# Rotary embedding on one core: tiles of 4 to 12 rows per partition in contiguous runs, with three tables made by TensorE

## The chip, the cores and the metric

One Trainium2 chip, one of its NeuronCores. The metric is the device time of one execution in microseconds (us). The kernel before takes 161.24 us (median of three runs, 161.16 to 161.56).

## What is computed

`x` is 16 batches of 512 positions of 1024 floats, that is 16 heads of 64. Each head is split into halves x1 and x2 of 32, and every position has its own 32 cosines and sines:

```python
x = x.reshape(batch, seq, num_heads, head_dim)
x1, x2 = (x[..., :half_dim].copy(), x[..., half_dim:].copy())
cos = cos[None, :, None, :].copy()
sin = sin[None, :, None, :].copy()
rotated = np.concatenate([x1 * cos - x2 * sin, x1 * sin + x2 * cos], axis=-1)
```

Input and output have 33.55 MB each. A position takes three passes over its 1024 floats: t1 = x times cos, t2 = the swapped halves times (-sin, sin), and the addition of the two.

## The kernel before, in words

**Rows and tiles.** The 8192 positions are laid out as 64 rows u of 128 positions, one position per partition, 4 KB each. A tile is some rows per partition that are loaded and stored together. Batches 0, 1, 14 and 15 are tiles of 4 rows (a partition's piece is 16 KB, contiguous in memory); the other twelve batches go in pairs, six tiles of 8 rows, where a partition's piece is 32 KB and neighbouring partitions alternate between the two batches of the pair (`x2`, `o2`, L110, L111). The result is written over x in the buffer `x_sb`, a ring of 40 rows (RING, L43). The first 40 rows are loaded up front; a later tile goes where stored tiles lay.

**Tables.** cos and sin come into `stage` in the layout of a tile of 4 rows. The layout of a pair needs each position's partner row, so TensorE makes it: `pick`, a 0/1 matrix that ACT spreads out of the identity (L178), is multiplied with `stage` into `pair_ps` (L209). ACT writes the signed sine tables `s1_sb` and `s2_sb` (L183 to L188). VectorE (DVE) copies two small tables for its own use (L280, L281).

**Who does what in a row.** The order on each engine is written out by hand, with waits on semaphores; an engine executes its own list in order.
- DVE multiplies t1 into one of three slots (NT1) of `t1_ps` in PSUM (L302), one row ahead (LEAD) of the additions. Row u takes the slot of row u-3 and waits until that row has been added.
- GpSimd (POOL) makes t2 (L263), one or two rows at a time, and waits for the tile's load. Row 3 of each 8-row tile is made by DVE itself (L295, flag V2).
- The addition is done by DVE (L313), or for the rows flagged PE2 (rows 1, 3 and 5 of 8) by TensorE: it adds t2 into PSUM by a matmul with the identity (L225), and the scalar engine (ACT) copies the slot back to `x_sb` (L192). That copy is called the evacuation below.
- SP waits until the last row of a tile is added and issues its store (L162). Stores run on the DMA queue q1.
- ACT issues all loads (L154), on the queue q10. The loads beyond the ring stand in ACT's own list between its evacuations: after a certain row, ACT waits until the stores of the rows to be overwritten have landed (L195) and then issues the load. LAG (L70) sets the row: the tile of batch 10 after row 17, that of batch 12 after row 25, batches 14 and 15 after row 33.

```python
later.setdefault((b * R1 - RING) // R2 * R2 + R2 - 1 + LAG, []).append(t)
...
for u in range(NU):
    if PE2[u]:
        ae.wait_ge(sem_e, n_pe[u])
        ae.activation(xs[:, u % RING, :], t1_ps[:, u % NT1, :], COPY).then_inc(sem_a, 1)
    for t in later.get(u, ()):
        k = (tiles[t][0] * R1 - RING) // R2
        ae.wait_ge(sem_out[k], 16 * stores_of(k))
        load(ae, t)
```

Of the kernel before, what the change touches and what calls it, by code (L numbers as in the profile page):

```python
# [6 lines left out]
def bass_split_heads_rope_kernel(  # L7
# [32 lines left out]
    singles = (0, 1, batch - 2, batch - 1)  # L40
    tiles = [(b, R1 if b in singles else R2) for b in range(batch) if b in singles or b % 2 == 0]
    NT = len(tiles)
    RING = 5 * R2  # L43
# [3 lines left out]
    EARLY = (NU - RING) // R2  # L47
# [3 lines left out]
    PE2 = [R1 <= u < NU - R1 and u % R2 in (1, 3, 5) for u in range(NU)]  # L51
    V2 = [tiles[t][1] == R2 and r == V_ROW for t, r in rows]
# [17 lines left out]
    LAG = 10  # L70

    with ExitStack() as stack:
# [3 lines left out]
        s1_sb = stack.enter_context(nc.sbuf_tensor([P, R1, 2, HALF], fp32))  # L76
        s2_sb = stack.enter_context(nc.sbuf_tensor([P, R2, 2, HALF], fp32))
        ident = stack.enter_context(nc.sbuf_tensor([P, P], fp32))
        pick = stack.enter_context(nc.sbuf_tensor([P, 2, P // 2, 2], fp32))
        zero = stack.enter_context(nc.sbuf_tensor([P, BANK], bf16))  # L80
        tab_ps = stack.enter_context(nc.psum_tensor([P, BANK], fp32))
        pair_ps = stack.enter_context(nc.psum_tensor([P, 2, 2, R1, HALF], fp32))
# [15 lines left out]
        sem_g = stack.enter_context(nc.semaphore("pick"))  # L98
# [3 lines left out]
        c1_ps = tab_ps[:, 0:R1 * HALF].rearrange("p (r d) -> p r d", d=HALF)  # L102
        v_ps = tab_ps[:, R1 * HALF:R1 * HALF + HD].rearrange("p (t d) -> p t d", d=HALF)

        def c_of(t, r):
            return c1_ps[:, r, :] if tiles[t][1] == R1 else pair_ps[:, r // R1, 0, r % R1, :]

        x1 = x.rearrange("b (s r) d -> b s (r d)", r=R1)
        o1 = out.rearrange("b (s r) h d -> b s (r h d)", r=R1)
        x2 = x.rearrange("b (s r) d -> s b (r d)", r=R2)  # L110
        o2 = out.rearrange("b (s r) h d -> s b (r h d)", r=R2)  # L111
        xs = x_sb[:].rearrange("p n h t d -> p n (h t d)")

        def in_dram(single, pairs, t):
            b, n = tiles[t]
            return single[b] if n == R1 else pairs[:, b:b + 2, :]

        def in_sbuf(t):
            b, n = tiles[t]
            k = b * R1 % RING  # L120
            return x_sb[:, k:k + n].rearrange("p n h t d -> p (n h t d)")
# [5 lines left out]
        def swapped(k):  # L127
            return x_sb[:, k, :, ::-1, :]

        def over_heads(table):  # L130
            return table[:, None, :, :].broadcast_to([P, H, 2, HALF])
# [17 lines left out]
        def stores_of(k):  # L149

            return sum(b * R1 // R2 == k for b, _ in tiles)

        def load(eng, t):
            eng.dma_start(in_sbuf(t), in_dram(x1, x2, t)).then_inc(sem_in[t], 16)  # L154

        def on_sync(sp):
            for u in range(NU):
                t, r, k = where(u)
                if r == tiles[t][1] - 1:
                    wait_added(sp, u)  # L160
                    k = u // R2
                    sp.dma_start(in_dram(o1, o2, t), in_sbuf(t)).then_inc(sem_out[k] if k < EARLY else sem_rest, 16)  # L162
            sp.wait_ge(sem_rest, 16 * sum(stores_of(k) for k in range(EARLY, NU // R2)))

        def on_scalar(ae):
            later = {}
            for t, (b, n) in enumerate(tiles):
                if b * R1 + n <= RING:
                    load(ae, t)
                else:  # L170

                    later.setdefault((b * R1 - RING) // R2 * R2 + R2 - 1 + LAG, []).append(t)
                if t == 0:
                    for i, (table, sem) in enumerate(((cos, sem_cos), (sin, sem_sin))):
                        ae.dma_start(stage[:, i, :], table.rearrange("(s r) d -> s (r d)", r=R1)).then_inc(sem, 16)  # L175

            ae.wait_ge(sem_i, 2)
            ae.activation(  # L178
                pick[:], ident[:].rearrange("q (s k) -> q k s", k=2)[:, :, :, None].broadcast_to([P, 2, P // 2, 2]), COPY
            ).then_inc(sem_g, 1)  # L180
            ae.wait_ge(sem_sin, 16)
            sv = stage[:, 1, :].rearrange("s (r d) -> s r d", d=HALF)
            ae.activation(s1_sb[:, :, 0, :], sv, COPY, scale=-1.0)  # L183
            ae.activation(s1_sb[:, :, 1, :], sv, COPY).then_inc(sem_s, 1)
            ae.wait_ge(sem_t, 2)
            s2 = s2_sb[:].rearrange("p (k r) t d -> p k r t d", r=R1)
            ae.activation(s2[:, :, :, 0, :], pair_ps[:, :, 1, :, :], COPY, scale=-1.0)  # L187
            ae.activation(s2[:, :, :, 1, :], pair_ps[:, :, 1, :, :], COPY).then_inc(sem_s, 1)  # L188
            for u in range(NU):
                if PE2[u]:  # L190
                    ae.wait_ge(sem_e, n_pe[u])
                    ae.activation(xs[:, u % RING, :], t1_ps[:, u % NT1, :], COPY).then_inc(sem_a, 1)  # L192
                for t in later.get(u, ()):
                    k = (tiles[t][0] * R1 - RING) // R2
                    ae.wait_ge(sem_out[k], 16 * stores_of(k))  # L195
                    load(ae, t)

        def on_tensor(pe):
            pe.wait_ge(sem_z, 1)
            for k in range(NT1):  # L200
                for b in range(EH):
                    pe.matmul(  # L202
                        t1_ps[:, k, b * BANK:(b + 1) * BANK], zero[:, 0:P], zero[:], start=True, stop=True
                    ).then_inc(sem_w, 1)
            pe.wait_ge(sem_g, 1)
            pe.wait_ge(sem_cos, 16)
            pe.wait_ge(sem_sin, 16)
            for k in range(2):
                pe.matmul(  # L209
                    pair_ps[:, k].rearrange("p c r d -> p (c r d)"),  # L210
                    pick[:, k].rearrange("q s b -> q (s b)"),
                    stage[:].rearrange("q c f -> q (c f)"),
                    start=True,
                    stop=True,
                ).then_inc(sem_t, 1)
            for u in range(NU):
                if not PE2[u]:
                    continue
                pe.wait_ge(sem_m, u + 1)

                if not V2[u]:
                    pe.wait_ge(sem_p, n_pool[u])
                t2 = t2_sb[:, u % NT2, :, :, :].rearrange("p h t d -> p (h t d)")
                for b in range(EH):
                    ins = pe.matmul(  # L225
                        t1_ps[:, u % NT1, b * BANK:(b + 1) * BANK],
                        ident[:],
                        t2[:, b * BANK:(b + 1) * BANK],
                        start=False,
                        stop=True,  # L230
                        skip_group_check=True,
                    )
                ins.then_inc(sem_e, 1)

        def on_gpsimd(pl):
# [3 lines left out]
                out=ident[:],  # L239
                in_=ident[:],  # L240
# [3 lines left out]
                pattern=[[-1, P]],  # L244
                channel_multiplier=1,
            ).then_inc(sem_i, 1)
            for u in range(NU):
# [4 lines left out]
                if (t, r) == (0, 0):  # L252
                    pl.wait_ge(sem_s, 1)
                if (t, r) == (2, 0):
                    pl.wait_ge(sem_s, 2)
# [6 lines left out]
                table = (s1_sb if tiles[t][1] == R1 else s2_sb)[:, r:r + n]  # L262
# [7 lines left out]
        def on_vector(ve):  # L270
            ve.memset(zero[:], 0.0).then_inc(sem_z, 1)  # L271
            ve.wait_ge(sem_cos, 16)
            ve.tensor_copy(c1_ps, stage[:, 0, :].rearrange("s (r d) -> s r d", d=HALF)).then_inc(sem_c, 1)  # L273
# [3 lines left out]
            def pair_tables():  # L277
                ve.wait_ge(sem_s, 2)
                row = pair_ps[:, V_ROW // R1, 1, V_ROW % R1, :]
                ve.tensor_scalar_mul(v_ps[:, 0, :], row, -1.0).then_inc(sem_c, 1)  # L280
                ve.tensor_copy(v_ps[:, 1, :], row).then_inc(sem_c, 1)  # L281

            first_v = V2.index(True)

            def mul(u):
# [3 lines left out]
                if (t, r) == (2, 0):  # L289
                    pair_tables()  # L290
                if u == first_v:
                    ve.wait_ge(sem_c, 3)
                if V2[u]:
                    wait_t2_free(ve, u)
                    ve.tensor_tensor(t2_sb[:, u % NT2, :, :, :], swapped(k), over_heads(v_ps), mult)  # L295
                if u >= NT1:
                    v = u - NT1
                    if PE2[v]:
                        ve.wait_ge(sem_a, n_pe[v])  # L299
                    else:  # L300
                        ve.wait_ge(sem_v, n_comb[v])
# [7 lines left out]
            def comb(u):  # L309
                t, r, k = where(u)  # L310
                ve.wait_ge(sem_m, u + 1)
                ve.wait_ge(sem_p, n_pool[u])  # L312
# [51 lines left out]
```

## Time and profile before

| | |
|---|---|
| median of three runs | 161.24 us |
| span of the profiled execution, first to last instruction | 159.6 us |
| DVE busy | 129.6 us (81%), 117 instructions |
| POOL busy | 131.7 us (82%), 41 instructions |
| PE busy | 64.4 us (40%), mean granted clock 0.764 |
| ACT busy | 24.3 us (15%) |
| DMA | 67.25 MB in 3169 packets, mean 421 GB/s |
| one multiplication or addition of a row on DVE | 1.22 us, the next one starts 1.13 us after it |
| t2 on POOL, two rows / one row | 4.53 / 2.36 us |
| last store, issue to landing | 7.7 us |

The span is what the profiler saw of one execution; the 1.6 us between it and the median lie outside its first and last instruction. In the profile's rows of 40 slices each digit is the busy share of 4 us in tenths. In the timeline a row is start, duration, engine, line and operation, and in brackets how long the engine was idle before it and what released it. "ACTq" and "SPq" are instructions that issue transfers or wait in the sequencer; "issue" as releaser means that the profile shows nothing the engine waited for.

### The profile page before, as it was taken

The numbers are of one execution on the slowest core, as the hardware profiler recorded it, in microseconds if no ns is written. First come the engines' busy times: TensorE is split into PE (matmuls) and PEld (weight loads), VectorE is DVE, ScalarE is ACT, GpSimd is POOL, SyncE is SP. The second block draws the span as 40 slices with busy tenths as digits, with TensorE's granted clock in tenths as the row PEclk, the third lists the DMA queues.
The fourth block names the chain that finished last, engine by engine and source line by source line (L and its number), as shares of the span: only waits on it lengthen the run. The fifth ranks groups of instructions, "written<-read, shape, count | busy, mean of one in ns | idle before, by whom it ended". The sixth has DMA issues, their size and how long they took to land.

```text
span 159.6 us, 499 instructions
## 1 busy us (share of the span) xinstructions
PE 64.4 (40%) x94; PEld 22.2 (14%) x94; DVE 129.6 (81%) x117; ACT 24.3 (15%) x27; POOL 131.7 (82%) x41
## 2 busy tenths in 40 slices
PE   6050017076408870789067400575058506900000
PEld 1020011021102220222021100211021102300000
DVE  0069947999999989998999629999999999556900
ACT  0420002004300250023102040023202310220000
POOL 1069999999999999999999798992999999089400
PEclk9999999759985589557759985589957995585555
DMA  5999999999999999999999999999999999999997
GB/s 144 396 466 472 394 411 431 448 476 402 394 448 406 495 419 402 476 435 402 443 435 435 394 476 435 402 460 394 427 456 448 443 394 423 472 419 435 386 456 300
DMA packets 3169, 67.25 MB, mean 421 GB/s; under 512 B 352, under 2 KB 608, under 8 KB 608
## 3 DMA queue, kind: packets, MB, share of 16 engines
q10 hardware_dynamic: 1728, 33.69, 49.8%
q1 hardware_dynamic: 1440, 33.56, 48.9%
q14 instruction: 1, 0.01, 0.0%
HBM read 33.69 MB, written 33.55 MB: 421 GB/s over the span
## 4 chain that ended last, share of the span: by engine, by line
DMA 61%; DVE 17%; POOL 5%; PE 5%; issue 4%; ACTq 1%; ACT 1%; DVEq 0%; POOLq 0%; SPq 0%
DMA x_sb<-in_x_dram 43%; DMA out_dram<-x_sb 18%; DVE t_ps L302 8%; DVE x_sb L313 7%; POOL t_sb L263 5%; PE t_ps L225 5%; DVE t_sb L295 2%; ACT x_sb L192 1%; ACTq L154 1%; ACTq L175 1%; DVE tab_ps L280 0%; DVEq L312 0%; DVE tab_ps L281 0%; DVEq L299 0%; POOLq L259 0%
## 5 line engine op out<-in xcount | busy, mean ns | idle before, releaser
L263 POOL TENSOR_TENSOR t_sb<-x_sb,s_sb 128x2048 f32<-128x2048 f32 (+1 forms) x35 | 131.0, 3784 | 17.1 <-DMA x_sb<-in_x_dram 8.3
L225 PE MATMUL t_ps<-t_sb,ident 128*128 128x512 f32 x84 | 59.6, 857 | 69.1 <-DVE t_ps L302 56.7
L302 DVE TENSOR_TENSOR t_ps<-x_sb,pair_ps 128x1024 f32<-128x1024 f32 x48 | 57.5, 1221 | 5.2 <-ACT x_sb L192 5.2
L313 DVE TENSOR_TENSOR x_sb<-t_ps,t_sb 128x1024 f32<-128x1024 f32 x43 | 52.2, 1216 | 5.9 <-POOL t_sb L263 5.9
L192 ACT ACTIVATE x_sb<-t_ps 128x1024 f32<-128x1024 f32 x21 | 21.4, 1024 | 107.6 <-PE t_ps L225 99.9
L225 PEld LDWEIGHTS t_ps<-t_sb,ident 128*128 128x128 f32 x84 | 20.3, 267 | 108.2 <-DVE t_ps L302 78.7
L302 DVE TENSOR_TENSOR t_ps<-x_sb,tab_ps 128x1024 f32<-128x1024 f32 x16 | 19.2, 1222 | 2.6 <-DMA x_sb<-in_x_dram 2.5
L295 DVE TENSOR_TENSOR t_sb<-x_sb,tab_ps 128x1024 f32<-128x1024 f32 x6 | 7.3, 1209 | 0.0
L273 DVE COPY tab_ps<-stage 128x128 f32<-128x128 f32 x1 | 0.3, 296 | 7.6 <-DMA stage<-in_cos_dram 7.6
L209 PE MATMUL pair_ps<-stage,pick 128*128 128x256 f32 x4 | 2.0, 667 | 5.1 <-DMA stage<-in_sin_dram 5.1
L202 PE MATMUL t_ps<-zero 128*128 128x512 bf16 x6 | 2.7, 629 | 1.3 <-DVE zero L271 1.3
L178 ACT ACT_TABLE_LOAD x1 | 1.3, 1283 | 5.5 <-issue 5.5
L209 PEld LDWEIGHTS pair_ps<-stage,pick 128*128 128x128 f32 x4 | 1.2, 324 | 6.1 <-issue 6.0
L202 PEld LDWEIGHTS t_ps<-zero 128*128 128x128 bf16 x6 | 0.7, 136 | 2.4 <-DVE zero L271 1.2
L271 DVE MEMSET zero<- 128x256 uint32 x1 | 0.3, 272 | 0.9 <-PEq L346 0.9
L187 ACT ACTIVATE s_sb<-pair_ps 128x256 f32<-128x256 f32 x1 | 0.4, 384 | 1.7 <-PE pair_ps L209 1.7
L183 ACT ACTIVATE s_sb<-stage 128x128 f32<-128x128 f32 x1 | 0.3, 310 | 1.8 <-DMA stage<-in_sin_dram 1.8
L236 POOL MEMSET ident<- 128x128 f32 x1 | 0.2, 205 | 0.3 <-POOLq L346 0.3
L178 ACT ACTIVATE pick<-ident 128x256 f32<-128x256 f32 x1 | 0.4, 416 | 0.0
L188 ACT ACTIVATE s_sb<-pair_ps 128x256 f32<-128x256 f32 x1 | 0.4, 377 | 0.0
L238 POOL TENSOR_SCALAR_AFFINE_SELECT ident<-ident 128x128 f32<-128x128 f32 x1 | 0.3, 295 | 0.1
L346 POOL MEMSET const-float32-0.0<- 128x1 f32 x1 | 0.1, 99 | 0.3 <-issue 0.3
(6 smaller groups left out, 1.0 us busy)
## 6 DMA issues: line engine op xcount, KB each, us to landing
x_sb<-in_x_dram ACTq DMA_DIRECT2D x6, 4096.0 KB, 38.7
out_dram<-x_sb SPq DMA_DIRECT2D x6, 4096.0 KB, 25.3
x_sb<-in_x_dram ACTq DMA_DIRECT2D x4, 2048.0 KB, 22.7
out_dram<-x_sb SPq DMA_DIRECT2D x4, 2048.0 KB, 16.1
stage<-in_cos_dram ACTq DMA_DIRECT2D x1, 64.0 KB, 7.5
stage<-in_sin_dram ACTq DMA_DIRECT2D x1, 64.0 KB, 7.2
```

The source lines that it names most:

```text
L154: eng.dma_start(in_sbuf(t), in_dram(x1, x2, t)).then_inc(sem_in[t], 16)
L175: ae.dma_start(stage[:, i, :], table.rearrange("(s r) d -> s (r d)", r=R1)).then_inc(sem, 16)
L178: ae.activation(pick[:], ident[:].rearrange("q (s k) -> q k s", k=2)[:, :, :, None].broadcast_to([P, 2, P // 2, 2]), COPY).then_inc(sem_g, 1)
L187: ae.activation(s2[:, :, :, 0, :], pair_ps[:, :, 1, :, :], COPY, scale=-1.0)
L192: ae.activation(xs[:, u % RING, :], t1_ps[:, u % NT1, :], COPY).then_inc(sem_a, 1)
L202: pe.matmul(t1_ps[:, k, b * BANK:(b + 1) * BANK], zero[:, 0:P], zero[:], start=True, stop=True).then_inc(sem_w, 1)
L209: pe.matmul(pair_ps[:, k].rearrange("p c r d -> p (c r d)"), pick[:, k].rearrange("q s b -> q (s b)"), stage[:].rearrange("q c f -> q (c f)"),
L225: ins = pe.matmul(t1_ps[:, u % NT1, b * BANK:(b + 1) * BANK], ident[:], t2[:, b * BANK:(b + 1) * BANK], start=False, stop=True, skip_group ...
L263: pl.tensor_tensor(t2_sb[:, u % NT2:u % NT2 + n], x_sb[:, k:k + n, :, ::-1, :], table[:, :, None, :, :].broadcast_to([P, n, H, 2, HALF]), ...
L295: ve.tensor_tensor(t2_sb[:, u % NT2, :, :, :], swapped(k), over_heads(v_ps), mult)
L302: ve.tensor_tensor(t1_ps[:, u % NT1, :].rearrange("p (h d) -> p h d", d=HALF), x_sb[:, k, :, :, :].rearrange("p h t d -> p (h t) d"), c_of ...
L313: ve.tensor_tensor(xs[:, k, :], t1_ps[:, u % NT1, :], t2_sb[:, u % NT2, :, :, :].rearrange("p h t d -> p (h t d)"), add,).then_inc(sem_v, 1)
```

## The change

The 64 rows become eight tiles of 4, 8, 8, 8, 12, 12, 8 and 4 rows, called tiles 0 to 7 in the following. Each tile is one contiguous run of positions across batch borders, and a partition's piece is 16, 32 or 48 KB, contiguous. The ring stays at 40 rows, so tiles 0 to 4 are loaded up front; tile 5 lies over tiles 0 and 1, tile 6 over tile 2, tile 7 over rows of tile 3. The late loads stand after rows 17, 25 and 33 (LATE), and each waits for the stores of the tiles under it. Loads 0 to 7 and stores 0 to 7 are those of the tiles.

In a tile of 8 rows a partition now holds 8 successive positions, in one of 12 rows 12, so with the tiles of 4 rows three table layouts are needed. The identity is laid out three times side by side, and TensorE multiplies its columns with a stride of 2 or 3 by `stage`. The tables of the 8-row tiles go through the third slot of `t1_ps`, those of the 12-row tiles through `tab_ps`. TensorE adds rows 1, 3 and 5 of an 8-row tile and rows 1, 3, 5 and 9 of a 12-row tile, 20 rows in all (21 before). On DVE the waits for its own earlier additions are dropped, and a multiplication waits for the multiplication before it.

The diff, cut to its core:

```diff
-    singles = (0, 1, batch - 2, batch - 1)
-    tiles = [(b, R1 if b in singles else R2) for b in range(batch) if b in singles or b % 2 == 0]
-    RING = 5 * R2
+    sizes = (R1, 2 * R1, 2 * R1, 2 * R1, 3 * R1, 3 * R1, 2 * R1, R1)
+    starts = [sum(sizes[:t]) for t in range(len(sizes))]
+    tiles = list(zip(starts, sizes))
+    RING = 10 * R1
...
-    EARLY = (NU - RING) // R2
+    over = [[j for j in range(t) if tiles[j][0] < u0 + n - RING and u0 - RING < tiles[j][0] + tiles[j][1]] for t, (u0, n) in enumerate(tiles)]
+    EARLY = 1 + max(max(o) for o in over if o)
...
-    PE2 = [R1 <= u < NU - R1 and u % R2 in (1, 3, 5) for u in range(NU)]
-    V2 = [tiles[t][1] == R2 and r == V_ROW for t, r in rows]
+    ON_PE = {R1: (1,), 2 * R1: (1, 3, 5), 3 * R1: (1, 3, 5, 9)}
+    PE2 = [0 < t < NT - 1 and r in ON_PE[tiles[t][1]] for t, r in rows]
+    V2 = [tiles[t][1] > R1 and r == V_ROW for t, r in rows]
...
-    LAG = 10
+    LATE = {5: 17, 6: 25, 7: 33}
...
+        def pieces(flat, t):
+            u0, n = tiles[t]
+            return flat[u0 * P:(u0 + n) * P, :].rearrange("(p r) d -> p (r d)", r=n)
...
         def load(eng, t):
-            eng.dma_start(in_sbuf(t), in_dram(x1, x2, t)).then_inc(sem_in[t], 16)
+            eng.dma_start(in_sbuf(t), pieces(xf, t)).then_inc(sem_in[t], 16)
...
-            ae.wait_ge(sem_i, 2)
-            ae.activation(
-                pick[:], ident[:].rearrange("q (s k) -> q k s", k=2)[:, :, :, None].broadcast_to([P, 2, P // 2, 2]), COPY
-            ).then_inc(sem_g, 1)
...
+            ae.wait_ge(sem_t, 1)
+            signed(2 * R1, spread_ps[:, :, 1])
+            ae.activation(two_ps.rearrange("p (j r) d -> p j r d", r=R1), spread_ps[:, :, 0], COPY).then_inc(sem_s, 1)
+            signed(3 * R1, group_ps[:, 2:3, 1], 2).then_inc(sem_s, 1)
             ae.wait_ge(sem_t, 2)
+            signed(3 * R1, group_ps[:, 0:2, 1]).then_inc(sem_s, 1)
...
-                for t in later.get(u, ()):
-                    k = (tiles[t][0] * R1 - RING) // R2
-                    ae.wait_ge(sem_out[k], 16 * stores_of(k))
-                    load(ae, t)
+                for t in range(NT):
+                    if LATE.get(t) == u:
+                        for j in over[t]:
+                            ae.wait_ge(sem_out[j], 16)
+                        load(ae, t)
...
+            for j in range(2):
+                spread(2 * R1, j, spread_ps[:, j])
+            spread(3 * R1, 2, group_ps[:, 2]).then_inc(sem_t, 1)
+            pe.wait_ge(sem_m, R1)
+            for j in range(2):
+                ins = spread(3 * R1, j, group_ps[:, j])
+            ins.then_inc(sem_t, 1)
...
-                if u >= NT1:
-                    v = u - NT1
-                    if PE2[v]:
-                        ve.wait_ge(sem_a, n_pe[v])
-                    else:
-                        ve.wait_ge(sem_v, n_comb[v])
+                if u >= NT1 and PE2[u - NT1]:
+                    ve.wait_ge(sem_a, n_pe[u - NT1])
+                if u >= 1 and not (u >= NT1 and PE2[u - NT1] and PE2[u - 1]):
+                    ve.wait_ge(sem_m, u)
```

## The prediction

> **What bounds the kernel now.** I read the page's engine and DMA rows first, then the DMA view by windows, then the timeline of DVE and ACT around the later loads, then the chain. On the page, the 40 slices and the queue rows:
>
> ```profile
> DVE  0069947999999989998999629999999999556900
> POOL 1069999999999999999999798992999999089400
> DMA  5999999999999999999999999999999999999997
> q10 hardware_dynamic: 1728, 33.69, 49.8%
> q1 hardware_dynamic: 1440, 33.56, 48.9%
> ```
>
> The DMA engines are full from the second slice to the last but one: loads (q10, issued by ACT) and stores (q1, by SP) take 49.8 + 48.9 = 98.7% of 16 engines. DVE and POOL have holes, and these cost nothing while a store waits in its queue. So this kernel is bound by bytes, and anything that leaves both queues empty adds to the time one for one.
>
> The DMA view of 26 to 37 us, when stores in 16 KB pieces run beside loads in 32 KB pieces:
>
> ```profile
> q10 hardware_dynamic: 96, 3.15, 66.6%
> q1 hardware_dynamic: 100, 1.64, 34.7%
> ```
>
> 96 packets against 100, though one kind is twice as large: an engine takes **one packet from each queue in turn**, a packet is a whole piece, and 11 us x 16 engines x 66.6% / 96 = 1.22 us for 32 KB, x 34.7% / 100 = 0.61 us for 16 KB (the packet records have 1.213 and 0.611 as medians). Each tile, whatever its size, is 128 pieces, 8 on each engine. So the time a store takes is set by the piece size of the load beside it: 32 beside 32 KB is 8 x 2 x 1.213 = 19.4 us from landing to landing; the stores of the DMA issues landed at 52.9, 72.7, 92.0 and 111.3, steps of 19.3 to 19.8.
>
> The timeline of ACT, ACT's queue and DVE between 83 and 100 us:
>
> ```profile
> 84.81 1.02 ACT L192 ACTIVATE x_sb<-t_ps 128x1024 f32<-128x1024 f32 x1 [8.29 <-PE t_ps L225]
> ...
> 92.04 1.53 ACTq L154 DMA_DIRECT2D x_sb<-in_x_dram  x2
> 93.61 1.94 ACT L192 ACTIVATE x_sb<-t_ps 128x1024 f32<-128x1024 f32 x2 [7.78 <-issue]
> 94.67 2.36 DVE L302 TENSOR_TENSOR t_ps<-x_sb,pair_ps 128x1024 f32<-128x1024 f32 x2 [4.41 <-ACT x_sb L192]
> ```
>
> and the chain of waits just before:
>
> ```profile
> 63.81 28.21 DMA out_dram<-x_sb
> 92.02 0.02 issue
> 92.04 0.34 ACTq L154
> ```
>
> After row 33 ACT stops at the wait of its next load (L195) until a store has landed at 92.0; the evacuations (L192) queue behind it, DVE finds no free slot of t1_ps and idles 4.41 us. Today it is free, because stores are still queued. This is where the change bites.
>
> **The change, part by part.**
>
> *Bytes and packets.* Per engine before: 64 packets of 16 KB and 96 of 32; after: 32 of 16, 64 of 32, 32 of 48. No run here has 48 KB; 0.611 and 1.213 lie on a line with a fixed 0.009, so 1.815, against 3 x 0.611 = 1.833. Gain 0 to 0.3 us. Gaps between transfers of a queue (0.5 to 0.7 us in the packet records) are filled by the other queue: windows from 24 to 110 us show DMA shares of 1.00 to 1.02.
> The Trainium skill ("DMA: Bandwidth & Descriptors", SWDGE vs HWDGE vs iDMA) puts a packet at preferably 4096 B or less, with turns taken at packet boundaries; that would make shares equal by bytes, which is rival B below, 162 to 164 us instead of 171. The trace is against it: 96 packets against 100, at twice the bytes.
>
> *Tables.* Removed: one 0.42 us activation (pick). Added: three matmul groups ahead of tile 1 where there were two (2.05 us for two at L209, so 3.1), and three more small activations there (0.3 to 0.4 each): ready near 13.3 us. POOL works on tile 0 until 9.55 + 4 x 2.34 = 18.9, and the loads run on, so 0; without that cover up to 1.5 us. The second table matmuls and activations (2.05 + 0.8) end near 20 us, needed at row 28. The wider identity costs POOL under 1 us before 9 us, when it waits for sin: 0.
>
> *DVE.* One addition more (PE takes 20 rows, not 21): 1.13 us. Copies: 0.5 more. Waits on its own last multiplication, about two per 8 rows: not in the trace; bounds 0 and 0.3 each, I take 0.15 (1.22 duration less 1.13 spacing, plus a semaphore). The DVE waits dropped cost nothing in the trace, so 0 gained. Together some 3 us over the run, none on the path while DMA is full.
>
> *The waits of ACT for stores.* LATE puts the loads of tiles 5, 6, 7 behind rows 17, 25, 33, the same rows as before. But tile 5 (12 rows) lies over tiles 0 and 1, and store 1 is now 8 rows, starts later and runs beside 48 KB loads. Behind the wait stand the evacuations of rows 21, 29 and 37; DVE's multiplications of rows 24, 32 and 40 need these slots. DVE operations follow each other at 1.131 us.
>
> Step by step, in us:
> - Load 1: before, 2 MB landed at 13.8; 4 MB adds 8 x 0.61: 18.7. Row 4's multiplication (before 17.77) and with it store 0 shift: issue 21.1, first packet 3.7 later as before (20.19 to 23.87), 14 us beside 32 KB: done 38.8.
> - Store 1: row 4's addition stays at 23.4 (POOL sets it); 12 operations and 0.5 of copies and waits on: 37.5, issue 38.7. First packet between 40.2 and 42.4 (1.5 or 3.7 after issue); I take 41.3. Load 3 has one packet left then (43.7); the other seven of store 1 alternate with 48 KB: 7 x 3.03 = 21.2, its last one ahead of the partner. ACT sees it at about **64.8**.
> - Row 24: without the wait, 37.5 + 14 operations and 0.3 (tile 2) + 7 operations = 61.5. With it: 64.8, load issue 0.6, evacuation 1.1: 66.5. **Stall 5.0.**
> - Row 28 at 66.5 + 6 operations + 0.8 = 74.1 (load 4 landed near 68). Row 32 unstalled 74.1 + 8 operations = 83.1. Store 2 (issued at 54.8) runs wholly beside 48 KB: 64.8 + 8 x 3.03 = **89.0**. Row 32 at 90.7. **Stall 7.6.**
> - Row 40 unstalled: 90.7 + 13 operations + 0.6 = 106.0. Store 3: one packet beside 48, seven beside 32 KB: 89.0 + 3.0 + 7 x 2.43 = **109.0**. Row 40 at 110.7. **Stall 4.7.**
> - From there 43 operations (48.6) + 0.9 to the last addition: 160.2, end 161.4. Store 6 is issued eight operations earlier, 153.5; it starts at 154.7, lasts 9.7; store 7 adds 8 x 0.611 = 4.9: 169.3, and 0.4 to the end of the span as now (159.2 to 159.6): **169.7**.
>
> The other way round: DMA work is unchanged (159.6 - 0.3), plus what it stands still. Store 4 is issued at 113 and lasts 14.5, to 129 to 131; store 5 is issued only at 137.4 (row 51): 8 to 9 us empty; then 1.6 ahead of store 6 and about 1 around load 7. 159.3 + 10 to 11.5 = 169.3 to 170.8. Both ways agree.
>
> The span before is 159.6 in the profiled execution; the median of the three runs is 161.24, so 1.6 lie around the span. 169.7 + 1.6 = **171.3 us**.
>
> Bounds: the first packet of store 1 moves everything by 1.1 either way; a 48 KB packet slower by a tenth would add 15 x 0.18 = 2.7; my gaps at the end are worth 1. Own range 168.9 to 173.6.
>
> **Rivals.**
>
> *B, 48 KB pieces don't hold the engine (they are cut, or served in equal bytes): the change doesn't do what it says.* Then stores 1 and 2 land before ACT is needed and those stalls go. But load 4 now lands late: 36 rows of loads and 20 of stores after 8.5 us, 56 x 1.213 = 67.9: 76.4, seen at 77, where row 28 was due at 69.1. 64 operations and 1.4 of waits on, the last addition is at 150.8, end 152.0; stores 6 and 7 as above: 145.3 + 9.7 + 4.9 + 0.4 = 160.3, up to 162.5 if the late stores start as slowly as store 0. Time 162 to 164. For it: nothing in the trace has a piece over 32 KB. Against: 32 KB goes whole, and 16 and 32 alternate one to one.
>
> *C, not slower: the DMA never runs empty.* One mechanism: the stores ahead of the three late loads land early enough. Place: ACT's waits. Store 5 has to be issued by about 128, when store 4 ends, instead of 137.4; so it decides where the three stalls together cost 17.3 - 9.4 = 8 us, and store 3 lands near 100 instead of 109. Then 161.24 - 0.3 = 160.95. For it: today's wait at row 33 costs DVE 4.41 us and the kernel nothing. Against: stores land at the pace of the packets beside them.
>
> *D, faster: fewer transfers, less fixed cost.* 16 data transfers instead of 20; if every one bared its gap of 0.7 us, 2.8 us fewer: 158.4. Against: the DMA share is 1.00 and above in every middle window.
> The Trainium skill ("DMA: Bandwidth & Descriptors", Anatomy of one DMA) gives 2.0 us fixed for each DMA; by it, four fewer would save 8 us, an estimate of 153 us. The trace disagrees: the gaps are covered.
>
> **How the numbers follow.** About 0.3% (0.5 us) is what a measurement of this kernel can tell from no change. My sum (A) 0.73, B 0.15, above 173.8 0.05 (48 KB packets slower than the line), C 0.05, D 0.02. The range 162.0 to 173.8 takes in A and B. Slower 0.93 (A, B and the case above), same 0.05 (C), faster 0.02 (D).
>
> **What would show it.** A right: the DMA row has holes near 130 to 138 and 153; DVE idles three times on ACT x_sb for 4 to 8 us, and ACT's first evacuation after each late load has a long "issue" idle; load 5 is issued near 65, load 6 near 89, load 7 near 109; 48 KB packets take 1.8 us. B: packets under 48 KB, loads 5 and 6 issued near 57 and 75, and one long POOL and DVE wait for load 4. C: a DMA row without holes. I am wrong if stores beside 48 KB loads land in under 20 us.

## The result, and the profile after

The changed kernel takes **172.54 us** (median of six runs, 171.52 to 173.38) against 161.28 us (161.16 to 161.56) for the kernel before in the same job: a ratio of 1.0698, 95% interval 1.0669 to 1.0726. The forecast was 171.3. The profiled execution took 173.17 us with a span of 170.7, so 2.5 us lie around the span where it was 1.6. Now and then an execution of one of these kernels takes some per cent longer (of the kernel before, 163.69, 165.59 and 169.15 us are on record); such executions are left out, which leaves one of six of `e10_eights`, and its other five are named beside it.

The page of the kernel after, its 40 slices and the queue rows:

```profile
DVE  0089879999999950699929997099999999999900
POOL 2079999999999995398956999069999999994000
DMA  6989899999899999999999999999998049885988
q10 hardware_dynamic: 1440, 33.69, 47.9%
q1 hardware_dynamic: 1152, 33.55, 46.0%
```

The same bytes go in fewer packets, but the DMA row has holes now. A slice is 4.27 us: the 8, 0, 4 in slices 31 to 33 are 128 to 141 us, and the 5 in slice 37 is 153.5 to 158. DVE and POOL have three more gaps well before, around slices 16, 21 and 26, that is near 65, 87 and 108 us. The busy time by windows gives the holes their size (start and end, length, then each engine; the DMA share and its GB/s stand last):

```profile
113.00:131.00 18.00, 7.73 (x13) 2.71 (x14) 17.93 (x17) 3.07 (x3) 17.99 (x5) 0.78 1.02 412
131.00:139.00 8.00, 3.60 (x4) 0.99 (x4) 7.63 (x7) 1.02 (x1) 8.00 (x3) 0.71 0.14 61
139.00:152.00 13.00, 9.94 (x12) 3.38 (x12) 12.65 (x12) 3.07 (x3) 13.00 (x4) 0.63 1.12 484
152.00:156.00 4.00, 0.00 (x0) 0.00 (x0) 4.00 (x5) 0.00 (x0) 3.38 (x2) 0.51 0.31 131
```

From 131 to 139 us the DMA share is 0.14 while DVE and POOL work almost without a pause: both queues are empty, because store 4 is done and store 5 isn't computed yet. In the packet records (start and duration of each piece that an engine moved) the 16 engines stand still for 6.3 us on average there, 1.9 near 154 and 0.3 near 111: 8.5 us in all. In the kernel before it is 0.02 us from 9 to 150 us.

Why DVE is late there shows in the timeline of ACT and its queue:

```profile
68.27 0.34 ACTq L163 DMA_DIRECT2D x_sb<-in_x_dram  x1
68.65 1.94 ACT L197 ACTIVATE x_sb<-t_ps 128x1024 f32<-128x1024 f32 x2 [16.65 <-DMA out_dram<-x_sb]
...
88.56 0.33 ACTq L163 DMA_DIRECT2D x_sb<-in_x_dram  x1
88.94 1.94 ACT L197 ACTIVATE x_sb<-t_ps 128x1024 f32<-128x1024 f32 x2 [11.84 <-DMA out_dram<-x_sb]
...
109.68 0.33 ACTq L163 DMA_DIRECT2D x_sb<-in_x_dram  x1
110.06 1.02 ACT L197 ACTIVATE x_sb<-t_ps 128x1024 f32<-128x1024 f32 x1 [12.68 <-DMA out_dram<-x_sb]
```

and in the timeline of DVE:

```profile
69.71 2.49 DVE L326 TENSOR_TENSOR t_ps<-x_sb,tab_ps 128x1024 f32<-128x1024 f32 x2 [7.43 <-ACT x_sb L197]
...
90.00 2.49 DVE L326 TENSOR_TENSOR t_ps<-x_sb,tab_ps 128x1024 f32<-128x1024 f32 x2 [3.72 <-ACT x_sb L197]
...
111.18 1.23 DVE L326 TENSOR_TENSOR t_ps<-x_sb,tab_ps 128x1024 f32<-128x1024 f32 x1 [5.62 <-ACT x_sb L197]
```

Three times ACT idles 12 to 17 us for a landing (`DMA out_dram<-x_sb`), issues its load, and does the evacuation that stood behind; about 1 us later DVE goes on, after 7.43, 3.72 and 5.62 us: 16.8 in all (18.2 with five short waits). The pace of the landings comes from the turns of the queues, here the DMA view of the kernel after from 44 to 64 us, when store 1 (32 KB pieces, q1) runs beside load 4 (48 KB pieces, q10):

```profile
q10 hardware_dynamic: 110, 5.21, 60.1%
q1 hardware_dynamic: 109, 3.57, 42.7%
```

110 packets against 109: one to one, whole pieces (4 of the 110 are small ones, of under 512 B, that end a load). The packet records have a median of 1.815 us for 48 KB.

### The profile page after: what moved, and what is told of

The parts are those of the page before. It is cut to its first block, busy times and chain, and to the rows that moved or that the text cites. A ratio compares the mean times of both kernels' runs of the same rounds, so it can differ in the third digit from the quotient of the medians.

```text
span 170.7 us, 461 instructions
## 1 busy us (share of the span) xinstructions
PE 70.9 (42%) x96; PEld 24.7 (14%) x96; DVE 132.7 (78%) x119; ACT 24.0 (14%) x30; POOL 132.2 (77%) x41
## 4 chain that ended last, share of the span: by engine, by line
DMA 39%; DVE 31%; POOL 11%; PE 7%; issue 4%; ACT 3%; ACTq 1%; DVEq 0%; POOLq 0%; SPq 0%
DMA out_dram<-x_sb 35%; DVE t_ps L326 19%; POOL t_sb L279 11%; DVE x_sb L339 10%; PE t_ps L242 7%; DMA stage<-in_sin_dram 4%; ACT x_sb L197 3%; DVE t_sb L321 2%; ACTq L163 1%; ACTq L179 0%; DVE tab_ps L294 0%; ACT s L183 0%; ACT s L184 0%; DVE tab_ps L297 0%; DVEq L325 0%
## 5 line engine op out<-in xcount | busy, mean ns | idle before, releaser
L279 POOL TENSOR_TENSOR t_sb<-x_sb,s 128x2048 f32<-128x2048 f32 (+1 forms) x35 | 131.0, 3783 | 22.5 <-DVE t_ps L326 14.6
L326 DVE TENSOR_TENSOR t_ps<-x_sb,tab_ps 128x1024 f32<-128x1024 f32 x64 | 78.3, 1223 | 19.6 <-ACT x_sb L197 18.2
L242 PE MATMUL t_ps<-t_sb,ident 128*128 128x512 f32 x80 | 63.2, 943 | 67.9 <-DVE t_ps L326 63.2
L339 DVE TENSOR_TENSOR x_sb<-t_ps,t_sb 128x1024 f32<-128x1024 f32 x44 | 53.4, 1217 | 1.6 <-POOL t_sb L279 1.6
L197 ACT ACTIVATE x_sb<-t_ps 128x1024 f32<-128x1024 f32 x20 | 20.3, 1024 | 111.2 <-PE t_ps L242 70.0
L217 PE MATMUL tab_ps<-stage,ident 128*128 128x256 f32 x6 | 3.1, 661 | 4.7 <-DVE t_ps L326 4.7
L217 PE MATMUL t_ps<-stage,ident 128*128 128x256 f32 x4 | 2.0, 667 | 5.2 <-DMA stage<-in_sin_dram 5.2
L217 PEld LDWEIGHTS tab_ps<-stage,ident 128*128 128x128 f32 x6 | 1.8, 327 | 5.8 <-DVE t_ps L326 5.4
L217 PEld LDWEIGHTS t_ps<-stage,ident 128*128 128x128 f32 x4 | 1.2, 323 | 6.3 <-issue 6.1
L183 ACT ACTIVATE s<-tab_ps 128x128 f32<-128x128 f32 (+1 forms) x2 | 0.7, 333 | 5.5 <-PE tab_ps L217 5.5
L184 ACT ACTIVATE s<-tab_ps 128x128 f32<-128x128 f32 (+1 forms) x2 | 0.7, 331 | 0.0
## 6 DMA issues: line engine op xcount, KB each, us to landing
out_dram<-x_sb SPq DMA_DIRECT2D x2, 2048.0 KB, 13.9
```

The costliest lines, as they stand in the source:

```text
L183: ae.activation(view[:, :, :, 0, :], table, COPY, scale=-1.0)
L184: return ae.activation(view[:, :, :, 1, :], table, COPY)
L217: return pe.matmul(dst.rearrange("p c r d -> p (c r d)"), ident[:, j:j + n // R1 * (P - 1) + 1:n // R1], stage[:].rearrange("q c f -> q (c ...
L242: ins = pe.matmul(t1_ps[:, u % NT1, b * BANK:(b + 1) * BANK], ident[:, 0:P], t2[:, b * BANK:(b + 1) * BANK], start=False, stop=True, skip_ ...
L279: pl.tensor_tensor(t2_sb[:, u % NT2:u % NT2 + n], x_sb[:, k:k + n, :, ::-1, :], table[:, :, None, :, :].broadcast_to([P, n, H, 2, HALF]), ...
L326: ve.tensor_tensor(t1_ps[:, u % NT1, :].rearrange("p (h d) -> p h d", d=HALF), x_sb[:, k, :, :, :].rearrange("p h t d -> p (h t) d"), c_of ...
```

## The experiments

All are edits of the kernel after, but for `e8_before_lag20`. The question of the first four: are the 11 us the three waits in ACT's list (theory), and do their stalls add up (as the forecast's bound for rival C had it), or does only the last one set a date before which the last stores can't be computed (rival)?

**All three loads later.**

```diff
-    LATE = {5: 17, 6: 25, 7: 33}
+    LATE = {5: 23, 6: 31, 7: 41}
```

> The three late loads stand after rows 23, 31 and 41 instead of 17, 25 and 33; nothing else changes. If ACT's waits for stores are the cause, the evacuations of rows 21, 29 and 37 are no longer behind them, DVE loses under 2 us to ACT, the DMA queues never run empty and the time is about 161.0 us (159.3 span + 1.6). Rival (the 12-row tiles are too coarse: a tile of 6 MB lands late and is stored late, whatever ACT does): still above 168 us, with DVE or POOL waiting for x_sb loads. Rival (tables, copies and added waits on DVE cost the time): 172 us still.

Measured: 165.09 us (164.59 to 165.54), ratio 1.0228 (1.0201 to 1.0255), span 162.7. The loads are issued at 68.5, 87.5 and 109.3, as before this edit, but less stands behind them. The waits of DVE for ACT (total, times, longest), first of the kernel after, then of this one, and two windows of this one:

```profile
DVE t_ps L326 <- ACT x_sb L197: 18.2, 8, 7.4
```

```profile
DVE t_ps L326 <- ACT x_sb L197: 3.5, 4, 2.5
```

```profile
131.00:139.00 8.00, 5.68 (x11) 1.69 (x9) 7.96 (x8) 2.05 (x2) 8.00 (x3) 0.89 1.08 467
...
159.60:162.50 2.90, 0.00 (x0) 0.00 (x0) 0.00 (x0) 0.00 (x0) 0.00 (x0) 0.50 0.06 23
```

The stalls fall to 3.5 us and the hole at 131 to 139 is filled (share 1.08). So the waits are worth 7.4 us of the 11.3. The rest, 3.7, is something else, which neither theory had: from 159.6 us the share is 0.06, one engine of sixteen (1/16 = 0.0625). The others ended at 159.7 to 159.8, the last at 162.3. At every landing of a store from store 1 on (67.85, the next one 65.50) one engine is behind. A hole of 0.7 us near 144 remains too, and 2.5 us lie around the span, where the kernel before has 1.4.

**Only the last wait later.**

```diff
-    LATE = {5: 17, 6: 25, 7: 33}
+    LATE = {5: 17, 6: 25, 7: 41}
```

> Only the last late load moves, from row 33 to row 41. If only the date counts on which the last wait lets ACT go on, then the second wait decides now: row 32 is multiplied near 90 us as in the changed kernel, row 40 near 106 instead of 111, about 5 us less: 167 to 168 us, with a hole in the DMA row of about 3 us near 132 and 1.6 near 149. If the stalls of DVE add up, the gain is the third stall, 5.6 us: also 167. If the waits don't matter: 172.5.

Measured: 166.98 us (166.41 to 168.87, three executions), ratio 1.0374 (1.03 to 1.0447). DVE keeps the stalls of 7.91 and 3.78 us; the holes shrink to 3.7 us near 131 and 1.5 near 149. Both readings had foreseen about 167, so this run doesn't decide between them.

**Only the first two waits later.**

```diff
-    LATE = {5: 17, 6: 25, 7: 33}
+    LATE = {5: 23, 6: 31, 7: 33}
```

> The first two late loads move to rows 23 and 31, the last stays behind row 33. If the stalls add up, as my sum read, 7.4 + 3.7 us go and the time is 161 to 162 us. If the last wait sets a date (store 3 lands near 109 us because its packets alternate with the load beside it, however early it was issued), DVE arrives earlier and waits longer: its third stall grows from 5.6 to some 13 to 16 us and the time stays within 1 us of 172.5.

Measured: 172.92 us (172.58 to 173.09), ratio 1.0711 (1.0691 to 1.0732): nothing gained. The timeline of DVE in this kernel:

```profile
89.91 1.23 DVE L326 TENSOR_TENSOR t_ps<-x_sb,tab_ps 128x1024 f32<-128x1024 f32 x1 [3.39 <-ACT x_sb L197]
...
111.08 1.23 DVE L326 TENSOR_TENSOR t_ps<-x_sb,tab_ps 128x1024 f32<-128x1024 f32 x1 [13.03 <-ACT x_sb L197]
```

The third stall grows from 5.62 to 13.03 us and ends at the same time, 111.1 (111.2 in the kernel after). Store 3 was issued at 72.2 instead of 79.6, and its last engine was still done only at 109.3 (109.4 in the kernel after), because it queues behind store 2. **What single stalls cost doesn't add up.** The landing of store 3 is a date before which row 40 can't be multiplied; whatever time was won before it is waited away there. The waits of DVE for ACT sum to nearly the same as in the kernel after (18.2):

```profile
DVE t_ps L326 <- ACT x_sb L197: 17.6, 6, 13.0
```

`e2_only_last`, which keeps two stalls and drops the third, gains about 5 us (ratio 1.0374 instead of 1.0698).

**All three earlier.**

```diff
-    LATE = {5: 17, 6: 25, 7: 33}
+    LATE = {5: 9, 6: 17, 7: 25}
```

> All three late loads stand 8 rows earlier: after rows 9, 17 and 25. If ACT's waits are the cause, the cost grows: the evacuations of rows 13, 21 and 29 wait for stores 1, 2 and 3, the stores are issued later still, and the time is about 185 to 192 us, with a hole in the DMA row of over 10 us. If the waits were hidden and something else costs the 11 us: within 2 us of 172.5, or less, since the loads are issued earlier.

Measured: 198.19 us (197.64 to 198.62), ratio 1.228 (1.2244 to 1.2315), more than expected. The waits of DVE on ACT sum to 43.6 us, the longest 24.4. Two windows of this kernel:

```profile
126.00:139.50 13.50, 4.83 (x6) 1.18 (x4) 12.86 (x12) 2.05 (x2) 13.39 (x5) 0.50 0.00 1
154.50:164.50 10.00, 3.78 (x4) 1.17 (x4) 9.64 (x9) 1.02 (x1) 10.00 (x4) 0.67 0.08 34
```

Both queues are empty for 13 and for 10 us. The engines also stand still in the middle, 2.7 us between 60 and 70 and 4.1 between 85 and 120, which the expectation didn't have: ACT waits for stores that were issued only at 79.8 and 108.2, so loads 6 and 7 were issued only at 96.9 and 119.3.

**The 48 KB loads cut into 16 KB pieces**, the waits left where they are: if an engine sends one piece of each queue in turn, the stores beside them must land sooner, and load 4 later.

```diff
+        def cuts(t):
+            return 3 if tiles[t][1] == 3 * R1 else 1
...
+            w = R1 * H * HD
+            for j in range(cuts(t)):
+                c = slice(j * w, (j + 1) * w) if cuts(t) > 1 else slice(None)
+                eng.dma_start(in_sbuf(t)[:, c], pieces(xf, t)[:, c]).then_inc(sem_in[t], 16)
...
```

> The loads of the two 12-row tiles are issued as three transfers each, so that a piece is 16 KB instead of 48; the stores stay at 48 KB and the late loads stay behind rows 17, 25 and 33. If an engine takes one packet from each queue in turn, a store beside these loads gets three times the turns: load 5 is issued near 57 us instead of 68, load 6 near 71 instead of 88.6, load 7 near 98 instead of 109.7; DVE's waits for ACT go, but load 4 lands late (near 77 us) and DVE waits 7 to 11 us for it; the time is 163 to 165 us, holes in the DMA row near 130 and 146. If the shares go by bytes, or the size of a piece does not matter: loads 5, 6, 7 issued as in the changed kernel and 172 us.

Measured: 166.03 us (165.51 to 167.42), ratio 1.0303 (1.0268 to 1.0339). Loads 5, 6 and 7 are issued from 58.7, 75.4 and 101.0. The waits of DVE:

```profile
DVE tab_ps L300 <- DMA x_sb<-in_x_dram: 8.9, 1, 8.9
...
DVE t_ps L332 <- ACT x_sb L203: 0.8, 3, 0.3
```

Store 1 landed at 58 instead of 68, and DVE's stalls on ACT are gone; one wait of 8.9 us for load 4 stands in their place. That is the mechanism of the prediction's rival B, and its 162 to 164 is exceeded by 2 us. It isn't the end of `e1_later`: here the engines end together (the last 0.1 us after the median one), and they stand still for 2.3 us near 131 and 1.5 near 148.

**The sizes of before with all else of the change** (contiguous runs, new tables, DVE's changed waits):

```diff
-    sizes = (R1, 2 * R1, 2 * R1, 2 * R1, 3 * R1, 3 * R1, 2 * R1, R1)
+    sizes = (R1, R1) + 6 * (2 * R1,) + (R1, R1)
...
-    LATE = {5: 17, 6: 25, 7: 33}
+    LATE = {6: 17, 7: 25, 8: 33, 9: 33}
```

> The tile sizes of before (4, 4, six of 8, 4, 4 rows) in contiguous runs, with the tables made by strided columns of the identity, the shorter waits on DVE and 20 rows on PE; late loads behind rows 17, 25, 33, 33 as before. No 48 KB pieces, and tables of the 12-row layout only in part. If the sizes and their stores are the cause, the time is that of before within 0.5%: 160.8 to 161.8 us, late loads issued near 53, 73 and 92 us. If the other edits (tables, contiguous runs, waits, one row fewer on PE) cost something, it shows here: 163 us or more. If contiguous runs are faster in memory than pairs two batches apart: below 160.5.

Measured: 161.43 us (161.18 to 162.06, 12 runs), ratio 1.0008 (1.0000 to 1.0017). Its DMA row and the waits of its DVE:

```profile
DMA  5999999999999999999999999999999999999997
```

```profile
DVE t_ps L314 <- ACT x_sb L195: 6.2, 5, 5.1
```

No hole, although DVE waits 6.2 us for ACT: free, as in the kernel before. So contiguous runs, the waits on DVE and the tables (those of 12 rows are made only in part here) cost nothing that can be measured; the loss is in the sizes with their late loads.

**The late loads in SP's list**, after stores 2, 3 and 4, with the same waits for landings:

```diff
-    LATE = {5: 17, 6: 25, 7: 33}
+    LATE = {5: 2, 6: 3, 7: 4}
...
+                    for v in range(NT):
+                        if LATE.get(v) == t:
+                            for j in over[v]:
+                                sp.wait_ge(sem_out[j], 16)
+                            load(sp, v)
```

> The three late loads are issued by SP, after stores 2, 3 and 4, with the same waits for stores; ACT's list holds only evacuations. The dates on which the stores land stay bound to the same data, but no evacuation stands behind them. If the blocked ACT is the cause and not the late arrival of the loads: DVE waits under 2 us for ACT, no hole in the DMA row, 160.8 to 161.5 us. SP itself is now held until a store has landed, so store 3 could be issued later, and loads and stores share one queue and come one after the other; if that leaves gaps of 1 to 2 us at each change: 162 to 165 us. If the loads' late arrival is the cause: 168 us or more.

Measured: 165.0 us (164.08 to 165.12), ratio 1.021 (1.0188 to 1.0231). DVE waits 0.8 us for ACT, and the DMA row has no hole before 158 us. A window of this kernel:

```profile
158.50:162.30 3.80, 0.00 (x0) 0.00 (x0) 0.00 (x0) 0.00 (x0) 0.00 (x0) 0.50 0.19 82
```

Almost without a stall it ends like `e1_later`: for 3.8 us a few engines work and the others are done. So no wait of ACT is needed for this part; the question is now why the engines are out of step, that is, why some of the 16 end a transfer microseconds after the others.

**The kernel before with its late loads ten rows later.** Theory: a load queue that has run empty starts again slowly beside a busy store queue. Here it does run empty.

```diff
-    LAG = 10
+    LAG = 20
```

> The kernel before with LAG 20 instead of 10: the late loads stand after rows 27, 35 and 43, so each is issued near 72.6, 88 and 106 us, 1 to 2 us after the load queue has run empty at 70.8 (before: issued at 53.0 and 72.7, always one load ahead). Bytes, piece sizes and stores are the same, and a store is queued all the time. If it costs something that a queue runs empty and starts again (the first packets after the restart slow, and the 16 engines no longer in step, so that each landing waits for the last one), the time is 162 to 164.5 us and the completions of a transfer spread over 2 us or more between the engines (0.2 to 0.6 before). If only bytes and empty engines count: 161.3 to 161.6 us, the loads landing some 2 us later and nothing else.

Measured: 163.42 us (162.92 to 165.08), ratio 1.0147 (1.0111 to 1.0183). The load of batch 10 is issued at 71.7, its first packet starts near 75.8, and it lands at 97.2. A window of this kernel shows the rate behind it:

```profile
84.00:88.00 4.00, 2.73 (x5) 0.68 (x4) 4.00 (x5) 1.52 (x2) 4.00 (x2) 0.85 1.03 360
```

The engines count as full (1.03) and move 360 GB/s, where the page of before has a mean of 421. DVE waits 7.5 us for loads, and the last store is late. So later loads with an empty load queue cost 1.5% here. Of the 2.5 us between the last packets of the two kernels (161.7 against 159.2), about half is packets that take longer (25.1 us beyond the medians over all engines, against 6.0 in the kernel before: 1.2 us for each engine), and the rest is that the engines wait for the last stores near 156 (1.5 us). The run doesn't part what the empty queue does from what the later loads do. The last engine completes a transfer at most 1.9 us after the median one, not quite the 2 or more that this theory wanted.

**The load queue kept fed**: `e1_later` with 4 rows of load 5 sent once store 0 has landed.

```diff
+                if u == 17:
+                    ae.wait_ge(sem_out[0], 16)
+                    load(ae, 5, 0)
...
-                        load(ae, t)
+                        load(ae, t, 1 if t == 5 else None)
```

> The kernel with all late loads moved (rows 23, 31, 41), and load 5 cut in two: the 4 rows of a partition that lie over tile 0 are issued after row 17 (store 0 has landed by then), the other 8 after row 23 as in that run. The load queue no longer runs empty near 68 us. If the 2.5 us by which one engine ended after the others came from the restart of the empty queue, the completions of load 5, store 2 and the last store lie within 1 us over the engines, and what is left is a late load 5 (its 16 turns beside stores, landing near 101 us): 163 to 164 us. If the lag of one engine has another cause, it stays above 2 us and the time is 165 us or more.

Measured: 167.17 us (166.9 to 167.82), ratio 1.0376 (1.0358 to 1.0394). A miss: the last engine completes a store up to 4.5 us after the median one, load 5 lands only near 104, and DVE's wait for it is 9.3 us:

```profile
DVE t_ps L330 <- DMA x_sb<-in_x_dram: 10.2, 2, 9.3
```

An empty load queue is not the cause of the lag, or not the only one. At the end the engines are together again here (0.1 us); what this kernel loses, it loses where both queues are empty, 2.9 us near 132 and 1.8 near 149, since the last stores are computed late.

**Tiles of 8 rows and late loads late, without 48 KB pieces**, and then the same sizes with the rows 17, 25 and 33:

```diff
-    sizes = (R1, 2 * R1, 2 * R1, 2 * R1, 3 * R1, 3 * R1, 2 * R1, R1)
+    sizes = (R1,) + 4 * (2 * R1,) + (R1, 2 * R1, 2 * R1, R1, R1)
...
-    LATE = {5: 17, 6: 25, 7: 33}
+    LATE = {6: 23, 7: 31, 8: 33, 9: 41}
```

> Contiguous tiles of 4, 8, 8, 8, 8, 4, 8, 8, 4 and 4 rows, tables as in the changed kernel but for the 12-row layout, late loads after rows 23, 31, 33 and 41. Tile 1 has 8 rows as in the changed kernel, so store 1 is as large and as late, but no piece is over 32 KB. With the late loads moved, the kernel with 12-row tiles still took 165.1 us, with one DMA engine 2.5 us behind the others. If 48 KB pieces put the engines out of step, this one is free of it: completions of a transfer within 1.3 us over the engines, no hole in the DMA row, 160.9 to 161.7 us. If the larger store 1 and the late loads after it do it, the lag stays: 163.5 to 165.5 us.

Measured: 161.65 us in the profiled execution, 165.7 to 166.97 in the other five; the kernel before 161.36 beside it. In the profiled one the engines are in step (from store 1 on the last engine completes a store at most 0.83 us after the median one) and the DMA row has no hole. So a store 1 of 8 rows with late loads need not cost anything. The five longer executions were not profiled: whether their engines were out of step isn't known, and what they lose stays open.

```diff
-    LATE = {6: 23, 7: 31, 8: 33, 9: 41}
+    LATE = {6: 17, 7: 25, 8: 33, 9: 33}
```

> The same tiles of 4 and 8 rows with the late loads after rows 17, 25, 33 and 33, the positions of the kernel before and of the changed one. If the date on which the stores land decides, and not the row of the wait, the stores beside 32 KB loads land near 61, 76 and 85 to 95 us, before DVE needs the slots for long: DVE loses under 4 us to ACT, no hole, and the time is that of the run with rows 23, 31, 33 and 41 within 0.5 us (160.9 to 161.7 without lag). If the positions alone were the fault of the changed kernel, this one loses some 5 us or more against that run.

Measured: 165.39 us (164.88 to 165.66, four executions), ratio 1.0245 (1.0224 to 1.0266). DVE waits 6.7 us for ACT, the longest 5.0, more than the 4 foreseen. Two windows of this kernel:

```profile
152.00:156.50 4.50, 0.00 (x0) 0.00 (x0) 3.44 (x4) 0.00 (x0) 1.15 (x1) 0.50 0.63 269
161.00:163.00 2.00, 0.00 (x0) 0.00 (x0) 0.00 (x0) 0.00 (x0) 0.00 (x0) 0.50 0.10 41
```

For most stores from store 3 on the last engine is 2.5 to 4.6 us behind the median one here, so 48 KB pieces aren't needed for the lag; at the end it is 1.7, and the engines that are ahead stand still near 156 (1.9 us on average over all). The waits behind rows 17, 25 and 33 don't cost 11 us when no piece is larger than 32 KB: the two parts of the change make the loss together. What the waits alone cost here stays open.

**Where the store stream starts**: `e10_eights`, and SP holds store 0 back until load 2 has landed, so that it starts between two loads instead of in the middle of one.

```diff
+                    if t == 0:
+                        sp.wait_ge(sem_in[2], 16)
```

> The kernel with tiles of 4, 8, 8, 8, 8, 4, 8, 8, 4, 4 rows and late loads after rows 23, 31, 33, 41, whose executions took 161.65 us once and 165.7 to 167.0 us five times; the profiled one, at 161.65, had its 16 DMA engines in step. One thing is added: SP issues store 0 only when load 2 has landed, near 30 us, so that the stream of stores starts at a border between two loads, as it does in the kernel before (23.9 us, between the loads of batches 2 and 4), and not in the middle of load 2 (25.0 us, where each engine lost 0.45 us on one packet). If that start throws the engines out of step, nearly all executions take 161 to 162 us. If it has nothing to do with it, most of them take 165 to 167 us as before.

Measured: 162.09 us (161.8 to 162.56, all six runs), ratio 1.0056 (1.0038 to 1.0073). Every execution lies near the shortest of `e10_eights`. The last engine is at most 2.3 us behind the median one, 1.35 at the end, so the lag isn't gone. This is a hint that the start of the stores matters, and no more: only the one short execution of `e10_eights` was profiled, the two kernels ran on different chips (the kernel before took 161.4 and 161.3 beside them), and a later store 0 also moves the landings after it.

## Why the prediction was right, and where it was not

- **The bound.** Bytes bound the kernel before, and what leaves both queues empty is lost one for one: held. The engines stand still for 8.5 of the 11.1 us that the span grew. About 3 more are packets that take longer than the median of their size: 53.6 us over all engines against 6.0, which is 3.0 us for each engine. The share hides this: from 24 to 32 us it is 0.99 at 397 GB/s, and 1.05 at 446 GB/s in the kernel before. The sum had nothing for it (only a bound, 48 KB packets slower by a tenth), and its 10 to 11.5 us of standing still were too large by 1.5 to 3: these two errors cancel as well.
- **The mechanism (A).** ACT waits for a landing, the evacuations queue behind it, DVE stalls: held, at all three places. Pieces of 48 KB took 1.815 us, the estimate to the digit, and were served whole and one to one, which is against B.
- **The sum.** 16.8 us of stalls against 17.3, a span of 170.7 against 169.7, time 172.54 against 171.3. The single stalls are 7.43, 3.72 and 5.62 against 5.0, 7.6 and 4.7: the sum is so near because the first two errors cancel, which is luck. Of the 1.2 us, 0.9 is what lies around the span (2.5 instead of 1.6).
- **Store 1 seen at 64.8**: 68.27. This is the step that failed most, by 3.5: the first packet came at 42.5 and not 41.3 (1.2); the median engine was done at 66.1, as 42.5 + 23.5 gives, but the last one at 67.7 (1.6); and 0.6 passed until ACT issued its load. The median hides two groups. In the packet records a packet starts within 0.01 us of the end of its engine's last one, so they can be strung together engine by engine: eight engines took a 48 KB packet of load 4 ahead of their first packet of store 1 (44.3 to 44.5 instead of 42.5 to 43.1); they ended store 1 at 66.6 to 67.7, the other eight at 64.9 to 65.5. The working had every engine in the second group. A landing is the last engine's. The Trainium skill ("DMA: Bandwidth & Descriptors", Why a DMA increments its semaphore by 16 and not by 1) says that the engines finish independently and that only the full 16 means that all data has landed; the trace agrees, with 1.6 us between the median engine and the last.
- **Store 2 after 24.2 us**: 20.3. The working took load 5 to run beside all of it. But load 5 was issued 1.0 us after the last packet of load 4 had ended (67.3), and its first packet came at 71.8: store 2 had the engines alone for 4.5 us, time for 3.7 packets (4.5 / 1.213) instead of 1.5 beside 48 KB (4.5 / 3.03), which by this estimate saves 2.2 x 1.815 = 4.0. This error took back most of the first, so that load 6 was issued at 88.56 (89.0 foreseen) and load 7 at 109.68 (109.0). The dates of the last two loads were near because two slips of opposite sign met, not because each term was right. (Its mark of "under 20 us" for being wrong was missed by 0.3, for this reason.)
- **C's threshold, "the three stalls together cost 8 us"**: it doesn't decide. Stalls can't be taken off one by one: `e3_first_two` moved the first two waits out of the way, and DVE still waited 17.6 us for ACT. And `e1_later` and `e7_sp_loads`, with 3.5 and 0.8 us of such waits, are far under 8 and still take 165. What decides in the kernel after is when the last landing comes, against the row that stands behind it.
- **What undoing gives.** C's price of 160.95 took it that a DMA row without stalls ends as before. `e7_sp_loads` has next to no stall and takes 165.0. Engines out of step were in no case of the forecast; in the kernel after they hide, since the holes let them catch up (0.1 us between the median engine and the last at the end).
- **Tables, layout, DVE's waits.** Cost 0, as foreseen: `e6_sizes`, 1.0008.
- **D.** Not tested by itself, since `e6_sizes` has as many transfers as the kernel before. But there was nothing to gain: strung together engine by engine, the packet records of the kernel before show no gaps of 0.5 to 0.7 us between transfers; from 9 to 150 us the engines stand still for 0.02 us on average. The 2.0 us that the forecast takes from the Trainium skill ("DMA: Bandwidth & Descriptors", Anatomy of one DMA) is given there for transfers that GpSimd issues; those here come from SP and ACT.

## What to carry to other kernels

A wait for a transfer in the list of an engine that others depend on sets a release date for all that stands behind it: work out that date from the pace of the turns (packets per engine times the sum of the two piece sizes' packet times), and move the wait, not the work ahead of it. Larger pieces on one queue make the other queue's landings later, so piece sizes and the rows of such waits have to be set together. Where transfers bind, look at whether all 16 engines end together, and at the packet times, which a share near 1 hides, before the rest is put down to the schedule.

## What was not expected of the hardware

The engines fall out of step. By the packet records, the last of the 16 engines completes a store 0.2 to 0.6 us after the median one in the kernel before; in `e6_sizes` it is up to 1.25, in `e1_later` one engine is 2.3 to 2.9 us behind the next from 67 us to the end, in `e9_fed` and `e11_eights_early` the last is up to 4.5 and 4.6 behind the median. Each engine moves its own 4.2 MB, and none takes over another's (strung together, the records of `e1_later` give each engine the same bytes), so the last one sets the end: 2.6 us after the median one in `e1_later`, 3.4 in `e7_sp_loads`. Packet time beyond the medians, summed over engines after 9 us, is 6.0 us in the kernel before, 13.9 in `e1_later` and 53.6 in the kernel after. Of the 53.6, 8.2 fall in 20 to 30 us, where store 0 starts, 15.9 in 70 to 80, where load 5 starts, and 21.5 in 110 to 120, where load 7 and store 4 start. In `e1_later` the late engine got load 4 before store 1 and so was behind with its stores from there; then, as load 5 started, it had one 32 KB packet of 2.32 us instead of 1.21, at 72.7, and stood still for 1.2 us after it, nearly all that it lacks at the end. But in `e8_before_lag20` 12.4 us of such packet time fall in 84 to 88, where no transfer has its first packets. What makes a packet longer stays open. A start of the stores in the middle of a load isn't sufficient for the lag: the profiled execution of `e10_eights` starts so, at 389 GB/s from 24 to 32 us, and stays in step.

A queue that had run empty took 3.5 us (kernel after, 68.3 to 71.8) to 4.1 us (`e8_before_lag20` and `e1_later`) from the issue of a load to its first packet beside a busy store queue.
